# The end of global attention: two of VectorE's new jobs in the last two units

## The chip, the cores and the metric

The kernel runs on one core of a Trainium2 chip. A core has five engines that run their own instruction streams and wait for one another by semaphores: TensorE (PE in the profile: matmul, with its weight loads as PEld), VectorE (DVE), ScalarE (ACT), GpSimd (POOL) and SyncE (SP, which here issues all DMAs). The metric is the time of one execution on the device in microseconds, as a median of runs; lower is better.

## The reference, cut to what matters

Two layers of a diffusion block over 1024 latent tokens and 256 context tokens, width 1024. Each layer projects the normalised tokens into three groups of heads, multiplies each branch by its gate, and projects the concatenation back. The branch that matters here is the global attention: 8 query heads of 64 that share 2 key/value heads, over all 1280 keys.

```python
def dense_attn(q, k, v):
    s = jnp.einsum("bqkgd,bskd->bkgqs", q, k).astype(jnp.float32)
    p = jax.nn.softmax(s, axis=-1).astype(v.dtype)
    o = jnp.einsum("bkgqs,bskd->bqkgd", p, v)
    return o.reshape(o.shape[0], o.shape[1], -1)
...
for l in range(DEPTH):
    ...
    aq, ak, av, ag, bz, bg, nq, nk, nv, ng = jnp.split(h @ w_in[l], SPLIT_POINTS, axis=-1)
    ...
    a_out = global_gqa(aq, ak, av, ak_c, av_c)
    ...
    y = jnp.concatenate([a_out * silu(ag), b_out * silu(bg), n_out * silu(ng)], axis=-1) @ w_out[l]
    ...
    x = x + gate[:, None] * y
```

## The kernel before

Each layer goes through its stages in order: the input projection in parts, the neighbourhood attention in 128-token units, the global attention, and the output projection. The change is in the global attention, which is the same code in both layers.

**The work of a unit.** The global attention is cut into 8 units (`gunits`, made by `ga_unit`): 2 halves of the 1024 queries (512 each), times 2 key heads, times 2 pairs of query heads. A unit handles two heads, `hi` 0 and 1. Its 1280 keys are taken in 5 steps `kp` of 256 keys. Scores are computed transposed, with keys on the partitions and queries along the free axis.

- `scores(hi, kp)`: TensorE computes 256 keys by 512 queries into a 128x1024 PSUM tile (L1037 and L1038, `ps_w`, of which there are two). ScalarE turns it into weights with one exponential (L1040, tile `gp`). The weights of a head are then added up over the steps into `gacc`: step 1 adds the weights of steps 0 and 1 (L1045), steps 2, 3 and 4 add theirs to it (L1048). Steps 1 to 3 are added on GpSimd, step 4 on VectorE, and VectorE then folds the two halves of `gacc` (L1050). An addition is called here by its head and step: "head 1, step 3".
- `values(kp, i)`: TensorE multiplies the weights of one step, both heads, into the output tile `ps_c` (L1057). It is issued one step late, between the next step's two scores. After step 4, which comes in the next unit's step 0, ScalarE copies `ps_c` to `gosb` (L1061).
- `finish()`: issued for a unit in step 2 of the next one. TensorE sums `gacc` over the partitions with a matrix of ones (L1066); ScalarE takes the reciprocal as exp of minus ln (L1070, L1071); VectorE mends it by a Newton step (L1073, L1074) and multiplies by the gated output (L1076, tile `gt`); GpSimd multiplies the gate by `gosb` (L1075).
- `store_u`, the last step of `finish`, splits the result `gt` into a leading part and a rest for the output projection: ScalarE copies `gt` into `hh` in TensorE's rounded float32 (L823), and VectorE subtracts that from `gt` into `hl` (L824).

**The shifts.** The softmax's shift for each query comes from maxima that are computed ahead: matmuls into `ps_b` (L1011, L1016) and maxima on VectorE (L1012, L1017), spread over the units before. They run out in the seventh unit (number 6), so that units 6 and 7 have little or none of them.

**Buffers.** The `gp` and `gacc` tiles of all units share seven 128x1024 buffers (tag `prob`, `PB = 7`); an exponential can only write a buffer whose earlier weights have been read by TensorE and added by whichever engine adds them.

**Order.** TensorE runs the instructions in the order in which the code issues them; on the other engines a scheduler has placed them, and each engine runs its own list strictly in order, so that one instruction that waits holds back all behind it. After the last unit the output projection begins with the first block of `w_out`, which was split before the global attention (L1210, L1211 and L1213, `woh` and `wol`); the other seven blocks are loaded (L1188) and split into two parts by ScalarE (L291) and VectorE (L292).

Of the kernel before, what the change touches and what calls it, by code (L numbers as in the profile page):

```python
# [11 lines left out]
ALU = mybir.AluOpType  # L12
# [62 lines left out]
def hybrid_block_kernel(  # L75
# [8 lines left out]
    PE, ACT, DVE, POOL, SP = nc.tensor, nc.scalar, nc.vector, nc.gpsimd, nc.sync  # L84

    def pool(name, bufs=1, space=None, side=None):
        kw = {}
        if space is not None:
            kw["space"] = space
        if space is not DRAM:  # L90
            kw["reuse_waits"] = "tile"
        if side is not None:
            kw["side"] = side
        return tc.tile_pool(name=name, bufs=bufs, **kw)
# [30 lines left out]
    def ps_one(name):  # L125
        wide.b += 1
        return ps_b[wide.b % 3]

    def ps_acc(name):
        return ps_c  # L130
# [241 lines left out]
    def load_parts(t, src, h, cols, top=0):  # L372

        for kind in range(2):
            i = kind ^ top
            SP.dma_start(out=t[i * 64:(i + 1) * 64].bitcast(F32), in_=head(src, h, kind, cols))

    for l in range(DEPTH):
# [114 lines left out]
        if l:  # L493
# [3 lines left out]
            for i in range(2):  # L497
                pr = ps_pair("ps_feat")
# [97 lines left out]
        for t in range(ntq):  # L596
            ps = proj_tok(W, t, 256)
            g = wp.tile([P, 512], F32, name="gate", bufs=2)
# [215 lines left out]
            g()  # L814


        def store_u(f, t0, n, u, eng=DVE):

            dst = hh[:, f, t0:t0 + n]
            if eng is POOL:  # L820
                POOL.tensor_copy(out=dst, in_=u)
            else:
                ACT.activation(out=dst, in_=u, func=AF.Copy)  # L823
            eng.tensor_tensor(out=hl[:, f, t0:t0 + n], in0=u, in1=dst.bitcast(F32), op=ALU.subtract)  # L824

        def pool_u(f, t0, n):
            u = ap_.tile([P, 512], F32, name="fin", tag="fin", bufs=4)
            SP.dma_start(out=u[:, :n], in_=upd[f, :, t0:t0 + n])
            store_u(4 + f, t0, n, u[:, :n])
# [147 lines left out]
        def gk(g):  # L977
            if g not in gks:
                gks[g] = load_gk(g)
            return gks[g]  # L980


        def ga_unit(cc, g, pr):
            f = 2 * g + pr
            cs = slice(cc * 512, (cc + 1) * 512)
            st = _Env()

            st.q1, st.q2 = (hh[:, f, cs], hl[:, f, cs]), [None] * 2
            st.p, st.acc = {}, [None] * 2

            def load():
                for hi in range(2):
                    load_parts(st.q1[hi], qad, 2 * f + hi, cs)

            def load2():
                for hi in range(2):
                    st.q2[hi] = ak_.tile([P, 512], F32R, name="gq", tag="q", bufs=QB)
                    load_parts(st.q2[hi], qad, 2 * f + hi, cs)

            def shift(i):  # L1000

                hi, j = divmod(i, 10)
                if i == 0:
                    load2()
                    st.mx = small.tile([P, 2, 4, 3], F32, tag="gmx", name="gmx")
                q1, mx = st.q1[hi], st.mx[:, hi]
                k1 = gk(g)[0]
                S = ps_one("ps_m")
                if j < 8:
                    qt, half = divmod(j, 2)  # L1010
                    PE.matmul(S, q1[:, qt * P:(qt + 1) * P], k1[:, half * 512:(half + 1) * 512], start=True, stop=True)  # L1011
                    DVE.reduce_max(out=mx[:, qt, half:half + 1], in_=S, axis=AX.X)  # L1012
                    return
                q0 = 2 * (j - 8)
                for i in range(2):
                    PE.matmul(S[:, i * 256:(i + 1) * 256], q1[:, (q0 + i) * P:(q0 + i + 1) * P], k1[:, SEQ:NT], start=True, stop=True)  # L1016
                DVE.reduce_max(out=mx[:, q0:q0 + 2, 2], in_=S.rearrange("p (a b) -> p a b", a=2), axis=AX.X)  # L1017
                if hi and j == 9:
                    st.nn = small.tile([P, 8], F32, tag="gnn", name="gnn")
                    DVE.tensor_reduce(out=st.nn, in_=st.mx.rearrange("p h q k -> p (h q) k"), op=ALU.max, axis=AX.X, negate=True)  # L1020

            def shift_rows():

                T = ps_one("ps_mt")
                PE.transpose(T[0:8, 0:P], st.nn, ident)
                r = ak_.tile([8, P], F32R, name="gmr", bufs=2)
                ACT.activation(out=r, in_=T[0:8, 0:P], func=AF.Copy)
                for hi in range(2):
                    SP.dma_start(out=st.q2[hi][0:1, :].rearrange("o (i p) -> o i p", p=P).bitcast(F32),
                                 in_=r[4 * hi:4 * hi + 4, :].bitcast(F32))  # L1030

            def scores(hi, kp):
                k1, k2 = gk(g)
                S = ps_pair("ps_st").rearrange("p (a b) -> p a b", a=2)
                for i in range(2):
                    kc = slice((2 * kp + i) * P, (2 * kp + i + 1) * P)
                    PE.matmul(S[:, i, :], k1[:, kc], st.q1[hi], start=True, stop=False)  # L1037
                    PE.matmul(S[:, i, :], k2[:, kc], st.q2[hi], start=False, stop=True)  # L1038
                p = ap_.tile([P, 2, 512], F32, name="gp", tag="prob", bufs=PB)
                ACT.activation(out=p, in_=S, func=AF.Exp)  # L1040
                st.p[hi, kp] = p
                pf = p.rearrange("p a b -> p (a b)")
                if kp == 1:
                    st.acc[hi] = ap_.tile([P, 1024], F32, name="gacc", tag="prob", bufs=PB)
                    POOL.tensor_tensor(out=st.acc[hi], in0=st.p[hi, 0].rearrange("p a b -> p (a b)"), in1=pf, op=ALU.add)  # L1045
                elif kp > 1:
                    eng = DVE if kp == 4 else POOL
                    eng.tensor_tensor(out=st.acc[hi], in0=st.acc[hi], in1=pf, op=ALU.add)  # L1048
                if kp == 4:
                    DVE.tensor_tensor(out=st.acc[hi][:, 0:512], in0=st.acc[hi][:, 0:512], in1=st.acc[hi][:, 512:1024], op=ALU.add)  # L1050

            def values(kp, i):
                if kp == 0 and i == 0:
                    st.o = ps_acc("ps_go")
                kt = 2 * kp + i
                for hi in range(2):
                    PE.matmul(st.o[hi * 64:(hi + 1) * 64, :], av[:, kt, g * 64:(g + 1) * 64], st.p[hi, kp][:, i, :],  # L1057
                              start=(kt == 0), stop=(kt == NTT - 1))
                if kt == NTT - 1:
                    st.osb = ap_.tile([P, 512], F32, name="gosb", tag="fin", bufs=4)  # L1060
                    ACT.activation(out=st.osb, in_=st.o, func=AF.Copy)  # L1061

            def finish():
                s_ps = ps_one("ps_gs")
                for hi in range(2):
                    PE.matmul(s_ps[hi * 64:(hi + 1) * 64, :], ones, st.acc[hi][:, 0:512], start=True, stop=True)  # L1066
                gt = ap_.tile([P, 512], F32, name="ggate", tag="fin", bufs=4)
                SP.dma_start(out=gt, in_=agd[f, :, cs])
                r0 = ap_.tile([P, 512], F32, name="gr0", tag="fin", bufs=4)
                ACT.activation(out=r0, in_=s_ps, func=AF.Ln)  # L1070
                ACT.activation(out=r0, in_=r0, func=AF.Exp, scale=-1.0)  # L1071
                t1 = ap_.tile([P, 512], F32, name="gt1", tag="fin", bufs=4)
                DVE.tensor_tensor(out=t1, in0=s_ps, in1=r0, op=ALU.mult)  # L1073
                DVE.scalar_tensor_tensor(out=t1, in0=t1, scalar=-2.0, in1=r0, op0=ALU.add, op1=ALU.mult)  # L1074
                POOL.tensor_tensor(out=gt, in0=gt, in1=st.osb, op=ALU.mult)  # L1075
                DVE.scalar_tensor_tensor(out=t1, in0=t1, scalar=-1.0, in1=gt, op0=ALU.mult, op1=ALU.mult)  # L1076
                store_u(f, cc * 512, 512, t1)

            return shift, scores, values, finish, load, shift_rows

        gunits = [ga_unit(cc, g, pr) for cc in range(2) for g in range(2) for pr in range(2)]

        shifts = []
        for i, u in enumerate(gunits):
# [86 lines left out]
        op = opx.enter_context(pool(f"op{l}", side=left))  # L1171
# [48 lines left out]
        for t0, n in ochunks:  # L1220
# [4 lines left out]
            for i in range(n):  # L1225
# [13 lines left out]
                elif last and t == NTL - 1:  # L1239

                    for c0, w in ((0, 512), (512, 256), (768, 256)):
                        ps, cs = ps_one("ps_y"), slice(c0, c0 + w)
                        for k in range(KT):
                            a, b = hh[:, k, ts_], hl[:, k, ts_]
# [7 lines left out]
                else:  # L1252
                    ps, f = proj_out(t)
# [88 lines left out]
```

## Time and profile before

| | us |
|---|---|
| median of 3 runs (1530.3 to 1532.41) | 1530.85 |
| the profiled execution's own time | 1529.36 |
| its span, first to last instruction | 1527.6 |
| TensorE busy | 1467.3 |
| VectorE busy | 864.1 |
| ScalarE busy | 640.7 |
| GpSimd busy | 515.0 |

The time of an execution is 1.8 us longer than the span that the profile covers. Rows of a timeline give the start from the span's beginning, the length, the engine, the line, the operation, the tiles (written <- read), the shapes and how many equal instructions in a row were merged; brackets give the idle time of the engine just ahead and what ended it. A busy share is a mean over stages with different limits, so the stage that the change touches is read by its own rows. In layer 0 the two units concerned and their end lie at about 675 to 722 us of the span, in layer 1 at about 1387 to 1433 us.

### The profile page before, as it was taken

How to read it: one execution, taken by the hardware profiler on the slowest of the kernel's cores; microseconds unless marked ns; L12 is line 12 of the kernel's file. 1: busy time of each engine (PE TensorE's matmuls, PEld its weight loads, DVE VectorE, ACT ScalarE, POOL GpSimd, SP SyncE). 2: the span in 40 equal slices, each digit the busy share in tenths (PEclk: the TensorE clock that was granted, in tenths of full speed). 3: DMA queues.
4: the chain of work that ended last, by engine and by line, in shares of the span. 5: the costliest groups of instructions: out<-in, count | busy, mean ns of one | idle time of the engine just before them, and what ended most of it. 6: DMA issues, size and time to landing. Idle time of an engine off the chain costs nothing.

```text
span 1527.6 us, 22281 instructions
## 1 busy us (share of the span) xinstructions
PE 1467.3 (96%) x8001; PEld 1072.9 (70%) x8001; DVE 864.1 (57%) x1666; ACT 640.7 (42%) x1228; POOL 515.0 (34%) x618
## 2 busy tenths in 40 slices
PE   5999999999999999999999999999999999999999
PEld 3787777788888554544788888878778854544577
DVE  3645344541678678774533553464368768785522
ACT  4643232334676444444312452333466544444400
POOL 0233346000144565564001323460012265665200
PEclk9999999999999999999999999999999999999999
DMA  9447445437745201010512132343796301001331
GB/s 310 149 126 233 130 149 167 148 114 174 196 127 141 66 22 42 21 42 21 179 70 103 61 111 75 90 138 83 180 219 143 105 22 42 21 28 35 140 116 55
DMA packets 153039, 167.91 MB, mean 110 GB/s; under 512 B 35384, under 2 KB 112032, under 8 KB 152864
## 3 DMA queue, kind: packets, MB, share of 16 engines
q1 hardware_dynamic: 152928, 166.48, 37.3%
q8 instruction: 63, 1.03, 0.3%
q14 instruction: 48, 0.39, 0.1%
HBM read 126.45 MB, written 40.86 MB: 110 GB/s over the span
## 4 chain that ended last, share of the span: by engine, by line
PE 51%; DVE 8%; ACT 3%; DMA 2%; issue 2%; POOL 0%; SPq 0%; DVEq 0%; ACTq 0%; POOLq 0%
PE ps_c L1057 8%; PE ps_w L1210 4%; PE ps_w L1213 4%; PE ps_w L1211 4%; PE ps_w L1037 4%; PE ps_w L1038 3%; PE ps_w L423 3%; PE ps_w L424 3%; PE ps_w L422 3%; PE ps_b L1011 3%; DVE gt L1076 2%; DVE gmx L1012 1%; DVE gacc L1048 1%; PE ps_c L902 1%; PE ps_b L1016 1%
## 5 line engine op out<-in xcount | busy, mean ns | idle before, releaser
L1040 ACT ACTIVATE gp<-ps_w 128x1024 f32<-128x1024 f32 x160 | 162.5, 1022 | 190.7 <-PE ps_w L1038 155.1
L422 PE MATMUL ps_w<-wh,hh 128*128 128x512 f32 (+1 forms) x624 | 234.7, 376 | 1.3 <-ACT wh L291 1.3
L423 PE MATMUL ps_w<-wl,hh 128*128 128x512 f32 (+1 forms) x624 | 228.5, 366 | 1.0 <-DVE wl L292 1.0
L424 PE MATMUL ps_w<-wh,hl 128*128 128x512 f32 (+1 forms) x624 | 228.1, 366 | 0.0
L1012 DVE TENSOR_REDUCE gmx<-ps_b 128x1 f32<-128x512 f32 x256 | 171.9, 685 | 72.1 <-PE ps_b L1011 67.9
L1057 PE MATMUL ps_c<-gp,av 128*64 128x512 f32 x640 | 166.6, 614 | 10.2 <-ACT gp L1040 10.1
L1048 POOL TENSOR_TENSOR gacc<-gacc,gp 128x1024 f32<-128x1024 f32 x64 | 161.3, 2549 | 25.8 <-ACT gp L1040 25.5
L422 PEld LDWEIGHTS ps_w<-wh,hh 128*128 128x128 f32 x624 | 117.7, 189 | 25.2 <-issue 2.9
L423 PEld LDWEIGHTS ps_w<-wl,hh 128*128 128x128 f32 x624 | 117.5, 188 | 21.4 <-DVE wl L292 2.2
L424 PEld LDWEIGHTS ps_w<-wh,hl 128*128 128x128 f32 x624 | 117.3, 188 | 21.2
L1038 PE MATMUL ps_w<-gq,kst 128*128 128x512 f32 x320 | 126.7, 396 | 0.0
L1210 PE MATMUL ps_w<-woh,hh 128*128 128x512 f32 x272 | 109.4, 402 | 0.0
L643 DVE TENSOR_REDUCE qss<-sq 128x8 f32<-128x512 f32 (+2 forms) x58 | 31.2, 538 | 135.3 <-ACT sq L641 135.2
L1211 PE MATMUL ps_w<-wol,hh 128*128 128x512 f32 x272 | 107.5, 395 | 0.0
L1057 PEld LDWEIGHTS ps_c<-gp,av 128*64 128x64 f32 x640 | 42.9, 137 | 88.5 <-issue 66.5
L877 POOL TENSOR_SCALAR rg<-ngate,rr 128x64 f32<-128x64 f32 x88 | 28.6, 329 | 225.9 <-PE ps_b L890 106.0
L1045 POOL TENSOR_TENSOR gacc<-gp 128x1024 f32<-128x1024 f32 x32 | 75.8, 2370 | 49.8 <-ACT gp L1040 49.8
L292 DVE TENSOR_TENSOR wl<-wraw,wh 128x512 fp32r<-128x512 f32 (+1 forms) x96 | 66.6, 713 | 35.1 <-ACT wh L291 33.7
L1213 PE MATMUL ps_w<-woh,hl 128*128 128x512 f32 x272 | 85.6, 396 | 0.0
L874 ACT ACTIVATE prob<-ps_w,m 128x768 f32<-128x768 f32 (+2 forms) x88 | 72.7, 826 | 25.6 <-DVE m L861 12.5
L430 PE MATMUL ps_w<-hh,wh 128*128 128x512 f32 (+1 forms) x208 | 80.7, 388 | 0.8 <-ACT wh L291 0.8
L432 PE MATMUL ps_w<-hh,wl 128*128 128x512 f32 (+1 forms) x208 | 78.9, 379 | 0.0
(226 smaller groups left out, 2973.7 us busy)
## 6 DMA issues: line engine op xcount, KB each, us to landing
wmod<-in_w_mod_dram SPq DMA_DIRECT2D x48, 512.0 KB
wraw<-in_w_in_dram SPq DMA_DIRECT2D x64, 256.0 KB
gq<-qad SPq DMA_DIRECT2D x64, 128.0 KB
woraw<-in_w_out_dram SPq DMA_DIRECT2D x14, 512.0 KB
wraw<-in_w_in_dram SPq DMA_DIRECT2D x48, 128.0 KB
kst<-knd SPq DMA_DIRECT2D x16, 320.0 KB
qad<-qklo SPq DMA_DIRECT2D x18, 256.0 KB
qad<-qkhi SPq DMA_DIRECT2D x18, 256.0 KB
```

The source lines that it names most:

```text
L422: PE.matmul(ps[:, :n], a, wh[:, off:off + n], start=(k == 0), stop=False)
L423: PE.matmul(ps[:, :n], a, wl[:, off:off + n], start=False, stop=False)
L424: PE.matmul(ps[:, :n], b, wh[:, off:off + n], start=False, stop=(k == KT - 1))
L430: PE.matmul(ps[:, :n], wh[:, fs], hh[:, k, ts_], start=(k == 0), stop=False)
L1012: DVE.reduce_max(out=mx[:, qt, half:half + 1], in_=S, axis=AX.X)
L1038: PE.matmul(S[:, i, :], k2[:, kc], st.q2[hi], start=False, stop=True)
L1040: ACT.activation(out=p, in_=S, func=AF.Exp)
L1048: eng.tensor_tensor(out=st.acc[hi], in0=st.acc[hi], in1=pf, op=ALU.add)
L1057: PE.matmul(st.o[hi * 64:(hi + 1) * 64, :], av[:, kt, g * 64:(g + 1) * 64], st.p[hi, kp][:, i, :], start=(kt == 0), stop=(kt == NTT - 1))
L1210: PE.matmul(ps[:, i2, :], a, oh[:, cs], start=(k == 0), stop=False)
L1211: PE.matmul(ps[:, i2, :], a, ol[:, cs], start=False, stop=False)
L1213: PE.matmul(ps[:, i2, :], b, oh[:, i2 * 512:(i2 + 1) * 512], start=False, stop=(k == KT - 1))
```

## The change

Two things move to VectorE, in both layers.

1. The copy of the result into `hh` (L823) moves from ScalarE to VectorE for the units numbered 5 and 6, counting from 0. Their `finish` is issued in step 2 of the next unit, so the copies stand in units 6 and 7: the last two. Unit 7's own `finish`, which comes after the last unit, keeps its copy on ScalarE.
2. Additions of weights move from GpSimd to VectorE for head 1: all of steps 1, 2 and 3 in unit 7, and step 3 in unit 6. Step 4 was on VectorE before. Head 0 keeps its additions on GpSimd up to step 3.

```diff
-        def store_u(f, t0, n, u, eng=DVE):
+        def store_u(f, t0, n, u, eng=DVE, cp=None):
             dst = hh[:, f, t0:t0 + n]
-            if eng is POOL:
-                POOL.tensor_copy(out=dst, in_=u)
+            if eng is POOL or cp:
+                (cp or eng).tensor_copy(out=dst, in_=u)
             else:
                 ACT.activation(out=dst, in_=u, func=AF.Copy)
             eng.tensor_tensor(out=hl[:, f, t0:t0 + n], in0=u, in1=dst.bitcast(F32), op=ALU.subtract)
...
-        def ga_unit(cc, g, pr):
+        def ga_unit(n, cc, g, pr):
...
+            def add_eng(hi, kp):
+
+                return DVE if kp == 4 or (hi and (n == 7 or (n == 6 and kp == 3))) else POOL
+
             def scores(hi, kp):
...
-                    POOL.tensor_tensor(out=st.acc[hi], in0=st.p[hi, 0].rearrange("p a b -> p (a b)"), in1=pf, op=ALU.add)
+                    add_eng(hi, kp).tensor_tensor(out=st.acc[hi], in0=st.p[hi, 0].rearrange("p a b -> p (a b)"), in1=pf, op=ALU.add)
                 elif kp > 1:
-                    eng = DVE if kp == 4 else POOL
-                    eng.tensor_tensor(out=st.acc[hi], in0=st.acc[hi], in1=pf, op=ALU.add)
+                    add_eng(hi, kp).tensor_tensor(out=st.acc[hi], in0=st.acc[hi], in1=pf, op=ALU.add)
...
-                store_u(f, cc * 512, 512, t1)
+                store_u(f, cc * 512, 512, t1, cp=DVE if n in (5, 6) else None)
...
-        gunits = [ga_unit(cc, g, pr) for cc in range(2) for g in range(2) for pr in range(2)]
+        gunits = [ga_unit(4 * cc + 2 * g + pr, cc, g, pr) for cc in range(2) for g in range(2) for pr in range(2)]
```

How the instructions stand on each engine follows from a scheduler, so three places are shown. All are in layer 1's last two units; layer 0 reads the same. The line numbers after the change are higher by three or four: the exponential L1040 is L1044, the additions L1045 and L1048 are L1049 and L1051, the fold L1050 is L1053, and the lines of `finish` go up by three.

ScalarE before, from unit 7's exponentials of step 2 to its last one (the copy of unit 6's result is the row with `hh`):

```order
L1040 ACTIVATE gp<-ps_w_10537 128x1024
L1070 ACTIVATE gr_13099<-ps_b_71 128x512
L1071 ACTIVATE gr_13099<-gr_13099 128x512
L1040 ACTIVATE gp<-ps_w_10536 128x1024
L823 ACTIVATE hh<-gt_13102 128x512
L1040 ACTIVATE gp<-ps_w_10537 128x1024
L1040 ACTIVATE gp<-ps_w_10536 128x1024
L1040 ACTIVATE gp<-ps_w_10537 128x1024
L1061 ACTIVATE gosb<-ps_c 128x512
```

After the change, at the same place:

```order
L1044 ACTIVATE gp<-ps_w_10537 128x1024
L1073 ACTIVATE gr_13099<-ps_b_71 128x512
L1074 ACTIVATE gr_13099<-gr_13099 128x512
L1044 ACTIVATE gp<-ps_w_10536 128x1024
L1044 ACTIVATE gp<-ps_w_10537 128x1024
L1044 ACTIVATE gp<-ps_w_10536 128x1024
L1044 ACTIVATE gp<-ps_w_10537 128x1024
L1064 ACTIVATE gosb<-ps_c 128x512
```

Nothing stands any longer between the exponential of head 0, step 3 and that of head 1, step 3.

VectorE in unit 7, before: unit 6's end, and then the step-4 additions with their folds.

```order
L1073 TENSOR_TENSOR gt_13102<-ps_b_71,gr_13099 128x512
L1074 SCALAR_TENSOR_TENSOR gt_13102<-gt_13102,gr_13099 128x512
L1076 SCALAR_TENSOR_TENSOR gt_13102<-gt_13102,ggate 128x512
L824 TENSOR_TENSOR hl<-gt_13102,hh 128x512
L1048 TENSOR_TENSOR gacc<-gacc,gp 128x1024
L1050 TENSOR_TENSOR gacc<-gacc 128x512
L1048 TENSOR_TENSOR gacc<-gacc,gp 128x1024
L1050 TENSOR_TENSOR gacc<-gacc 128x512
```

After:

```order
L1049 TENSOR_TENSOR gacc<-gp 128x1024
L1051 TENSOR_TENSOR gacc<-gacc,gp 128x1024
L1076 TENSOR_TENSOR gt_13102<-ps_b_71,gr_13099 128x512
L1077 SCALAR_TENSOR_TENSOR gt_13102<-gt_13102,gr_13099 128x512
L1079 SCALAR_TENSOR_TENSOR gt_13102<-gt_13102,ggate 128x512
L821 CAST hh<-gt_13102 128x512
L824 TENSOR_TENSOR hl<-gt_13102,hh 128x512
L1051 TENSOR_TENSOR gacc<-gacc,gp 128x1024 x2
L1053 TENSOR_TENSOR gacc<-gacc 128x512
L1051 TENSOR_TENSOR gacc<-gacc,gp 128x1024
L1053 TENSOR_TENSOR gacc<-gacc 128x512
```

Head 1's additions of steps 1 and 2 stand ahead of unit 6's end, the copy (CAST) inside it, and head 1's step 3 behind it, ahead of head 0's step 4; in all, four more instructions ahead of the last fold.

GpSimd, units 6 and 7, before and then after:

```order
L1045 TENSOR_TENSOR gacc<-gp 128x1024 x2
L1048 TENSOR_TENSOR gacc<-gacc,gp 128x1024 x4
L1075 TENSOR_TENSOR ggate<-ggate,gosb 128x512
L1045 TENSOR_TENSOR gacc<-gp 128x1024 x2
L1048 TENSOR_TENSOR gacc<-gacc,gp 128x1024 x4
L1075 TENSOR_TENSOR ggate<-ggate,gosb 128x512
```

```order
L1049 TENSOR_TENSOR gacc<-gp 128x1024 x2
L1051 TENSOR_TENSOR gacc<-gacc,gp 128x1024 x3
L1078 TENSOR_TENSOR ggate<-ggate,gosb 128x512
L1049 TENSOR_TENSOR gacc<-gp 128x1024
L1051 TENSOR_TENSOR gacc<-gacc,gp 128x1024 x2
L1078 TENSOR_TENSOR ggate<-ggate,gosb 128x512
```

One addition has left unit 6, three have left unit 7. TensorE's and SyncE's lists are the same as before but for line numbers.

## The prediction

> **What bounds the kernel now.** First the page: TensorE is busy for 96% of the span, so time can only go where TensorE stands still.
>
> ```profile
> span 1527.6 us, 22281 instructions
> PE 1467.3 (96%) x8001; PEld 1072.9 (70%) x8001; DVE 864.1 (57%) x1666; ACT 640.7 (42%) x1228; POOL 515.0 (34%) x618
> ```
>
> Then TensorE's waits: the end of layer 0's global attention (640 to 725 us), that of layer 1's (1360 to 1434 us), and what follows layer 0's (722 to 1000 us). Columns: us in total, times, longest.
>
> ```profile
> PE ps_c L1057 <- ACT gp L1040: 5.0, 2, 3.1
> ...
> PE ps_c L1057 <- ACT gp L1040: 5.2, 3, 3.1
> PE ps_b L1066 <- DVE gacc L1050: 0.5, 1, 0.5
> ...
> PE ps_w L422 <- ACT wh L291: 0.8, 1, 0.8
> ```
>
> In each layer TensorE's products with the weights wait twice for ScalarE's exponential, and behind that it hardly waits. TensorE's timeline shows where; layer 1, and at the foot two rows of layer 0:
>
> ```profile
> 1395.31 1.07 PE L1057 MATMUL ps_c<-gp,av 128*64 128x512 f32 x2
> 1398.24 1.93 PE L1057 MATMUL ps_c<-gp,av 128*64 128x512 f32 x6 [1.86 <-ACT gp L1040]
> 1400.11 0.50 PE L1037 MATMUL ps_w<-hl,kst 128*128 128x512 f32 x1
> 1402.15 2.25 PE L1057 MATMUL ps_c<-gp,av 128*64 128x512 f32 x8
> 1414.87 0.49 PE L1037 MATMUL ps_w<-hh,kst 128*128 128x512 f32 x1
> 1419.90 1.07 PE L1057 MATMUL ps_c<-gp,av 128*64 128x512 f32 x2
> 1424.09 3.53 PE L1057 MATMUL ps_c<-gp,av 128*64 128x512 f32 x6 [3.11 <-ACT gp L1040]
> 1427.54 0.55 PE L1037 MATMUL ps_w<-hl,kst 128*128 128x512 f32 x1
> 1432.39 1.07 PE L1066 MATMUL ps_b<-gacc,ones 128*64 128x512 f32 x2 [0.49 <-DVE gacc L1050]
> 1433.39 0.50 PE L1210 MATMUL ps_w<-woh,hh 128*128 128x512 f32 x1
> ...
> 683.05 1.07 PE L1057 MATMUL ps_c<-gp,av 128*64 128x512 f32 x2
> 721.79 0.50 PE L1210 MATMUL ps_w<-woh,hh 128*128 128x512 f32 x1
> ```
>
> A group of eight L1057 that isn't held up takes 2.2 us (1402.15). The step-3 group of unit 6 is torn: two go at 1395.31, six at 1398.24. That of unit 7 is torn further, and its six take 3.53 instead of 1.93 us. ScalarE shows the cause:
>
> ```profile
> 1396.65 0.63 ACT L823 ACTIVATE hh<-gt 128x512 fp32r<-128x512 f32 x1 [4.07 <-DVE gt L1076]
> 1397.19 1.92 ACT L1040 ACTIVATE gp<-ps_w 128x1024 f32<-128x1024 f32 x2
> 1409.78 1.03 ACT L1040 ACTIVATE gp<-ps_w 128x1024 f32<-128x1024 f32 x1 [2.22 <-PE ps_w L1038]
> 1413.33 1.94 ACT L1040 ACTIVATE gp<-ps_w 128x1024 f32<-128x1024 f32 x2 [2.52 <-POOL gacc L1045]
> 1416.33 1.01 ACT L1040 ACTIVATE gp<-ps_w 128x1024 f32<-128x1024 f32 x1
> 1422.49 0.63 ACT L823 ACTIVATE hh<-gt 128x512 fp32r<-128x512 f32 x1 [5.15 <-DVE gt L1076]
> 1423.03 1.92 ACT L1040 ACTIVATE gp<-ps_w 128x1024 f32<-128x1024 f32 x2
> 1428.89 1.02 ACT L1040 ACTIVATE gp<-ps_w 128x1024 f32<-128x1024 f32 x1 [3.94 <-PE ps_w L1038]
> ```
>
> The copy L823 waits 4.07 and 5.15 us for VectorE's L1076, and head 1's step-3 exponential, whose scores have long been done, stands behind it. And L1076 is late because of GpSimd (VectorE's rows, then GpSimd's):
>
> ```profile
> 1416.46 0.69 DVE L1073 TENSOR_TENSOR gt<-ps_b,gr 128x512 f32<-128x512 f32 x1 [11.99 <-ACT gr L1071]
> 1417.18 2.52 DVE L1074 SCALAR_TENSOR_TENSOR gt<-gt,gr 128x512 f32<-128x512 f32 x1
> 1419.80 2.65 DVE L1076 SCALAR_TENSOR_TENSOR gt<-gt,ggate 128x512 f32<-128x512 f32 x1
> 1425.05 2.56 DVE L1048 TENSOR_TENSOR gacc<-gacc,gp 128x1024 f32<-128x1024 f32 x1 [1.20 <-ACT gp L1040]
> 1430.38 1.22 DVE L1048 TENSOR_TENSOR gacc<-gacc,gp 128x1024 f32<-128x1024 f32 x1 [2.05 <-ACT gp L1040]
> 1431.64 0.69 DVE L1050 TENSOR_TENSOR gacc<-gacc 128x512 f32<-128x512 f32 x1
> ...
> 1410.95 2.35 POOL L1045 TENSOR_TENSOR gacc<-gp 128x1024 f32<-128x1024 f32 x1 [0.94 <-ACT gp L1040]
> 1414.43 7.47 POOL L1048 TENSOR_TENSOR gacc<-gacc,gp 128x1024 f32<-128x1024 f32 x3 [1.14 <-ACT gp L1040]
> ```
>
> L1073, with one operand in PSUM, takes 0.69 us beside a busy GpSimd. L1074 and L1076, with both operands in SBUF, take 2.5 and 2.65, and L1076 ends 0.55 us after GpSimd's third addition (1421.90). The same addition on VectorE takes 2.56 us or, with GpSimd idle, 1.22. So the two take turns, a whole instruction at a time; L1074 and L1076 unhindered would take about 0.69. On GpSimd an addition takes 2.35.
>
> The granted clock (sixth figure, between busy times and DMA share) tells why the six were slow: after the 1.9 us of unit 6 it stays at 1.00, after the 3.1 us of unit 7 it falls to about half for some microseconds.
>
> ```profile
> 1389.00:1402.00 13.00, 11.13 (x43) 4.95 (x41) 9.84 (x9) 6.21 (x9) 9.43 (x4) 1.00 0.29 101
> 1424.00:1428.00 4.00, 3.92 (x8) 1.07 (x9) 2.92 (x2) 0.95 (x2) 2.35 (x1) 0.57 0.02 4
> 714.00:718.00 4.00, 4.00 (x7) 1.46 (x6) 2.08 (x2) 0.34 (x1) 0.31 (x1) 0.54 0.00 0
> ```
>
> **The change part by part.** Layer 1 first, in the times of this span.
>
> *Copy off ScalarE, unit 6.* The exponential of head 1, step 3 can go when its scores are done, about 1394.5 (they end ahead of the group at 1395.31), and ends at 1395.5. The group then runs through: 1395.3 + 2.2 = 1397.5, and the next scores start there instead of at 1400.11. Gain 2.6 us.
>
> *Copy off ScalarE, unit 7.* All is 2.6 earlier, so the group starts at 1417.3 and its exponential ends at about 1417.4. It ends at 1417.3 + 2.2 = 1419.5, where head 1's step-4 scores started at 1427.54: 8.0 us gained so far, of which 3.1 was the wait and 1.6 the halved clock.
>
> *Additions to VectorE, and the waits that they add.* In unit 7 the exponential of head 0, step 2 needs a buffer that head 1's step-1 addition has read. That was GpSimd's 1410.95 row, the 2.52 us wait of 1413.33. Now it is VectorE's: the weights end at 1408.2 (1409.78 + 1.03 - 2.6), 1.22 us make 1409.5, and the exponential runs until 1410.5. Behind it on ScalarE stand head 1's step 2 and unit 6's reciprocal. TensorE needs its PSUM tile for the scores at 1412.3 (1414.87 - 2.6): 1.8 us of cover. The other buffers that VectorE now frees are those of unit 6's head 1, done by about 1402, some 2 us and more ahead of use. If this cover went, each microsecond would be one on TensorE.
>
> *VectorE's tail.* This sets the end, since the last sums (L1066) need the last fold (L1050). GpSimd's last addition of unit 7, head 0's step 3, starts when its weights are there. Their scores start at 1412.3 and end some 1.1 later; with 1.0 of exponential that is 1414.5, and the addition ends at 1416.9. VectorE first adds head 1's step 2 (behind GpSimd's addition of head 0's step 2, 1410.5 to 1412.9), until 1414.2, then L1073 until 1414.9, when GpSimd is at work again: L1074 must wait, and ends at 1416.9 + 0.55 = 1417.45. From there GpSimd is idle and nothing is in the way. With 0.05 us between instructions: L1076 0.69 (1418.2), the copy 0.45 (1418.7), L824 0.69 (1419.45), head 1's step 3 1.22 (1420.7), head 0's step 4 1.22 (1421.95), its fold 0.69 (1422.7), head 1's step 4 1.22 (1423.95), the fold 0.69 (1424.7). From last fold to first L1210 it was 1433.39 - (1431.64 + 0.69) = 1.06 us; so L1210 starts at 1425.75. Gain in layer 1: 1433.39 - 1425.75 = 7.6 us.
>
> The copy's price has no row. The nearest above is a VectorE copy out of PSUM, below it an operation with one SBUF operand on twice the elements:
>
> ```profile
> L893 DVE COPY probt<-ps_b 128x512 f32<-128x512 f32 x16 | 10.8, 677 | 2.3 <-PE ps_b L890 2.2
> L256 DVE TENSOR_SCALAR xt<-xt,rs_y 128x1024 f32<-128x1024 f32 x10 | 7.2, 749 | 0.1
> ```
>
> Half of 749 ns is 0.37; so 0.37 to 0.68 us. I take 0.45, near L256, whose operands lie in the same memory. The other end costs 0.2 us a layer.
>
> *Layer 0.* The same order, 1395.31 - 683.05 = 712.26 us earlier, so L1210 would start at 1425.75 - 712.26 = 713.5 instead of 721.79: 8.3 us. It is more because the clock stayed low for longer there.
>
> *Behind the units.* The eight blocks of `w_out`, their splits and the output are released by what stands around the first L1210 and move with it; the only wait shown behind layer 0 was 0.8 us. I charge nothing; a gain lost there is a rival.
>
> Sum: 7.6 + 8.3 = 15.9 us. The profiled execution took 1529.36 (span 1527.6, and 1.8 around it), which makes 1513.5. The median before is 1530.85, 1.5 above that execution; against the median it is 1530.85 - 15.9 = 1514.9.
>
> **The rivals.** *VectorE gets its turn first* (0.11): L1074 slips in ahead of GpSimd's last addition, which it misses by about 0.5 us in my sum, and the tail is 2.4 us shorter. Then TensorE is the limit: the last exponential ends 1.35 + 1.02 us after the scores' start (1428.89 against 1427.54), at 1421.9; last products and sums bring L1210 to about 1424.5. Gain 8.9 + 9.5 = 18.4: 1512.4. Against it: GpSimd needs only the exponential, VectorE two operations.
>
> *VectorE loses one turn more, or the gain is lost in part later* (0.11): one more collision costs 2.35 us a layer and stretches TensorE's wait for the fold, about 1.2 us in my sum, to 3.5, past the 3.1 that halved the clock: 1.6 more. So 4 us a layer: 15.9 - 8 = 8 gained, 1523. If layer 0's or layer 1's gain were lost to a later `w_out` load, it would be 1523 as well.
>
> *VectorE becomes the bound* (0.04): if all seven two-operand instructions of the tail met GpSimd, four additions would cost 1.34 more each (2.56 - 1.22) and L1076 and L824 1.9 each: 9.2 us, L1210 at 1434.9 and 722.7, and the clock halved behind it, 1.6 a layer. That is 1.5 + 0.9 + 3.2 = 5.6 us slower, 1536.5. It decides from five or six collisions a layer; against it, GpSimd has only three additions left in unit 7, and is idle in the tail. [...]
>
> *Nothing comes of it* (0.02): another wait ends where the old did, 1530.5.
>
> **How the numbers follow.** The forecast, both torn groups whole and VectorE's tail as summed, has 0.72. The predicted time is its 1515, on its own 1513 to 1517 (the copy's bounds, and 1 us a layer for starts read off rows). The range runs from 1511, below the first rival, to 1521, the forecast with three more microseconds lost in each layer; it leaves out the second rival, the slower case and the one without gain, 0.17 together. Faster by over 0.2% (3 us, about what a measurement tells apart here) are forecast and the first two rivals, 0.94; within it 0.02; slower 0.04.
>
> **What would show it.** In the timeline after, the step-3 groups of units 6 and 7 should be whole (eight in 2.2 us), with no L823 between exponentials and the clock at 1.00. Unit 6's L1074 and unit 7's should still be stretched, the copy at about 0.45. TensorE's last wait for the fold should grow from 0.5 to about 1.2 us. The span from unit 6's group to L1210 should be 30.4 us in both layers (38.1 and 38.7 before). A torn group, or several additions of 2.5 us on VectorE behind unit 7's L1076, would make it wrong.

## The result, and the profile after

| | before | after |
|---|---|---|
| median of four runs each, side by side, us | 1531.63 (1530.3 to 1533.77) | 1514.60 (1511.32 to 1516.31) |
| the profiled execution's own time, us | 1529.36 | 1513.59 |
| from unit 6's step-3 group of products to the first matmul of the output projection, layer 0 | 38.74 | 30.14 |
| the same, layer 1 | 38.08 | 30.10 |

The ratio of the times is 0.9888, with a 95% interval from 0.987 to 0.9907. The change makes the kernel 1.1% faster, 17.0 us by these medians and 15.8 us by the two profiled executions.

The page after has TensorE 10.2 us less busy than before (1467.3), though it runs the same 8001 matmuls. In the two stretches of the table its busy time fell from 66.0 to 58.4 us: a torn group of products counts 3.0 us (1.07 + 1.93) where a whole one takes 2.2, and the halved clock makes up most of the rest. The other 2.6 us lie outside the stretches, mainly ahead of the first one, where the two executions differ without the change's doing.

```profile
span 1511.8 us, 22274 instructions
PE 1457.1 (96%) x8001; PEld 1071.0 (71%) x8001; DVE 866.0 (57%) x1678; ACT 639.5 (42%) x1224; POOL 495.6 (33%) x610
```

TensorE's waits after, for the same three stretches as before: the end of layer 0's global attention, that of layer 1's, and what follows layer 0's (us in total, times, longest).

```profile
PE ps_b L1069 <- DVE gacc L1053: 0.7, 1, 0.7
PE ps_c L1060 <- ACT gp L1044: 0.2, 1, 0.2
...
PE ps_b L1069 <- DVE gacc L1053: 0.8, 1, 0.8
PE ps_c L1060 <- ACT gp L1044: 0.2, 1, 0.2
...
PE ps_w L422 <- ACT wh L291: 0.9, 1, 0.9
```

The products' wait for the exponential was 5.0 and 5.2 us and is 0.2 in each layer. The last sums' wait for the fold has grown from 0.5 to 0.8 in layer 1; in layer 0, where none is listed before, it is 0.7. What follows layer 0 waits 0.9 where it waited 0.8, so nothing was given back there. TensorE's timeline, layer 1 and at the foot two rows of layer 0:

```profile
1387.52 2.18 PE L1060 MATMUL ps_c<-gp,av 128*64 128x512 f32 x8
1389.63 0.50 PE L1041 MATMUL ps_w<-hl,kst 128*128 128x512 f32 x1
...
1409.43 2.19 PE L1060 MATMUL ps_c<-gp,av 128*64 128x512 f32 x8
1411.55 0.50 PE L1041 MATMUL ps_w<-hl,kst 128*128 128x512 f32 x1
...
1416.62 1.07 PE L1069 MATMUL ps_b<-gacc,ones 128*64 128x512 f32 x2 [0.76 <-DVE gacc L1053]
1417.62 0.50 PE L1213 MATMUL ps_w<-woh,hh 128*128 128x512 f32 x1
...
683.58 2.19 PE L1060 MATMUL ps_c<-gp,av 128*64 128x512 f32 x8
713.72 0.50 PE L1213 MATMUL ps_w<-woh,hh 128*128 128x512 f32 x1
```

Both step-3 groups are whole: eight products in 2.2 us, where two went before and six after a wait. The granted clock (the sixth figure) stays at full speed through both ends, where it was at 0.54 and 0.57:

```profile
1405.00:1420.00 15.00, 14.06 (x53) 6.57 (x52) 12.05 (x12) 7.52 (x11) 3.95 (x3) 1.00 0.17 54
700.00:714.00 14.00, 13.10 (x49) 5.43 (x46) 11.74 (x11) 6.55 (x9) 5.05 (x3) 1.00 0.18 56
```

ScalarE's exponentials of steps 2 and 3 of unit 7 (the middle row is head 0, step 2, which needs a buffer; the last row is both heads of step 3, with nothing between them), then VectorE's list from unit 7's first addition to the last fold, and GpSimd's last addition:

```profile
1401.76 1.02 ACT L1044 ACTIVATE gp<-ps_w 128x1024 f32<-128x1024 f32 x1 [1.42 <-DVE gacc L1049]
1408.61 1.95 ACT L1044 ACTIVATE gp<-ps_w 128x1024 f32<-128x1024 f32 x2 [1.90 <-PE ps_w L1042]
...
1400.44 1.23 DVE L1049 TENSOR_TENSOR gacc<-gp 128x1024 f32<-128x1024 f32 x1 [5.28 <-ACT gp L1044]
1404.61 1.77 DVE L1051 TENSOR_TENSOR gacc<-gacc,gp 128x1024 f32<-128x1024 f32 x1 [2.94 <-ACT gp L1044]
1406.31 0.68 DVE L1076 TENSOR_TENSOR gt<-ps_b,gr 128x512 f32<-128x512 f32 x1
1407.02 2.78 DVE L1077 SCALAR_TENSOR_TENSOR gt<-gt,gr 128x512 f32<-128x512 f32 x1
1409.83 0.69 DVE L1079 SCALAR_TENSOR_TENSOR gt<-gt,ggate 128x512 f32<-128x512 f32 x1
1410.55 0.43 DVE L821 CAST hh<-gt 128x512 fp32r<-128x512 f32 x1
1411.01 0.69 DVE L824 TENSOR_TENSOR hl<-gt,hh 128x512 fp32r<-128x512 f32 x1
1411.62 2.35 DVE L1051 TENSOR_TENSOR gacc<-gacc,gp 128x1024 f32<-128x1024 f32 x2
1414.01 0.69 DVE L1053 TENSOR_TENSOR gacc<-gacc 128x512 f32<-128x512 f32 x1
1414.62 1.22 DVE L1051 TENSOR_TENSOR gacc<-gacc,gp 128x1024 f32<-128x1024 f32 x1
1415.87 0.69 DVE L1053 TENSOR_TENSOR gacc<-gacc 128x512 f32<-128x512 f32 x1
...
1406.85 2.39 POOL L1051 TENSOR_TENSOR gacc<-gacc,gp 128x1024 f32<-128x1024 f32 x1 [1.55 <-ACT gp L1044]
```

L1077 still waits for GpSimd's addition (it ends at 1409.80, the addition at 1409.24). Behind it GpSimd is idle up to 1416.56, and every VectorE instruction takes its unhindered time (0.69 us on 128x512, 1.2 on 128x1024). The copy, now a CAST on VectorE, takes 0.43 us.

The two gains, 8.60 and 7.98, make 16.6 us, 0.8 more than the executions differ by. The rest is outside: layer 0's stretch began 0.53 us later in the span (683.58 for 683.05), and the way from layer 0's first output matmul to layer 1's stretch took 673.80 for 673.52.

### The profile page after: what moved, and what is told of

Same layout as the page of the kernel before. It is cut to its first block, busy times and chain, and to the rows that moved or that the text cites. A ratio compares the mean times of both kernels' runs of the same rounds, so it can differ in the third digit from the quotient of the medians.

```text
span 1511.8 us, 22274 instructions
## 1 busy us (share of the span) xinstructions
PE 1457.1 (96%) x8001; PEld 1071.0 (71%) x8001; DVE 866.0 (57%) x1678; ACT 639.5 (42%) x1224; POOL 495.6 (33%) x610
## 4 chain that ended last, share of the span: by engine, by line
PE 52%; DVE 8%; DMA 2%; issue 2%; ACT 2%; SPq 1%; POOL 0%; DVEq 0%; ACTq 0%
PE ps_c L1060 8%; PE ps_w L1213 4%; PE ps_w L1216 4%; PE ps_w L1214 4%; PE ps_w L1041 4%; PE ps_w L1042 4%; PE ps_w L423 3%; PE ps_w L424 3%; PE ps_w L422 3%; PE ps_b L1011 3%; DVE gacc L1051 2%; DVE gmx L1012 1%; DVE gt L1079 1%; PE ps_c L902 1%; PE ps_b L1016 1%
## 5 line engine op out<-in xcount | busy, mean ns | idle before, releaser
L1044 ACT ACTIVATE gp<-ps_w 128x1024 f32<-128x1024 f32 x160 | 162.8, 1022 | 193.3 <-PE ps_w L1042 159.5
L1012 DVE TENSOR_REDUCE gmx<-ps_b 128x1 f32<-128x512 f32 x256 | 171.8, 685 | 72.1 <-PE ps_b L1011 67.9
L1060 PE MATMUL ps_c<-gp,av 128*64 128x512 f32 x640 | 159.8, 605 | 0.3 <-ACT gp L1044 0.3
L1051 POOL TENSOR_TENSOR gacc<-gacc,gp 128x1024 f32<-128x1024 f32 x58 | 146.5, 2552 | 24.3 <-ACT gp L1044 24.1
L1213 PE MATMUL ps_w<-woh,hh 128*128 128x512 f32 x272 | 109.5, 403 | 0.0
L1049 POOL TENSOR_TENSOR gacc<-gp 128x1024 f32<-128x1024 f32 x30 | 71.1, 2371 | 47.5 <-ACT gp L1044 47.5
```

Of the source, the lines that this page charges most:

```text
L1051: add_eng(hi, kp).tensor_tensor(out=st.acc[hi], in0=st.acc[hi], in1=pf, op=ALU.add)
L1213: PE.matmul(ps[:, i2, :], a, oh[:, cs], start=(k == 0), stop=False)
```

## The experiments

The theory: an exponential stood on ScalarE behind a copy that waited for VectorE, VectorE waited for GpSimd, and the second of these waits halved TensorE's clock (0.54 in layer 0, 0.57 in layer 1); the copy's move ends the waits, and the additions' move keeps VectorE from ending late. The rivals: the copy alone does it all, or the additions alone do; the halved clock is not a cost of its own; VectorE is now nearly the bound. "Stretch" below is that of the table above, in layer 0 and in layer 1. The runs of the first four experiments stood beside 18 runs of the kernel before (median 1530.93), those of the others beside 17 (1529.65).

**The copy alone.** The additions go back to where they were.

```diff
-                return DVE if kp == 4 or (hi and (n == 7 or (n == 6 and kp == 3))) else POOL
+                return DVE if kp == 4 else POOL
```

> Only the copy of the result goes to VectorE for units 5 and 6; all additions up to step 3 stay on GpSimd. The measure is the stretch from the start of unit 6's step-3 group of products to the first matmul of the output projection: 38.1 us in layer 1 and 38.7 in layer 0 before, 30.1 in both with the whole change. Theory (the copy on ScalarE tears the groups, the additions only set VectorE's tail): both groups whole, but L1077 and L1079 of unit 7 each wait for a GpSimd addition, the last fold comes some 2 us later and TensorE waits about 3 us for it: 32 to 33 us a layer, 10 to 13 us gained in all, some 1519. Rival one (the copy is everything): 30.1 a layer, 16 gained, 1515. Rival two (what helps is GpSimd's relief): a group is still torn, 36 a layer or more, under 5 gained.

Measured: 1524.81 us, ratio 0.9956 (0.9939 to 0.9972); stretch 34.51 and 33.57, so 4.2 and 4.5 us gained. The groups are whole, but the end is later than expected, and the time misses the expected 1519 by 6 us. VectorE and GpSimd in layer 1's unit 7:

```profile
1414.22 2.52 DVE L1077 SCALAR_TENSOR_TENSOR gt<-gt,gr 128x512 f32<-128x512 f32 x1
1416.84 2.67 DVE L1079 SCALAR_TENSOR_TENSOR gt<-gt,ggate 128x512 f32<-128x512 f32 x1
1419.55 2.47 DVE L821 CAST hh<-gt 128x512 fp32r<-128x512 f32 x1
...
1424.52 2.29 DVE L1051 TENSOR_TENSOR gacc<-gacc,gp 128x1024 f32<-128x1024 f32 x1
...
1411.47 10.27 POOL L1051 TENSOR_TENSOR gacc<-gacc,gp 128x1024 f32<-128x1024 f32 x4 [1.14 <-ACT gp L1044]
1424.08 1.65 POOL L1078 TENSOR_TENSOR ggate<-ggate,gosb 128x512 f32<-128x512 f32 x1 [2.34 <-ACT gosb L1064]
```

GpSimd runs four additions back to back, and VectorE gets one instruction in per addition: L1077, L1079 and the copy start 2.6 to 2.7 us apart. The copy takes 2.47 instead of 0.43. Even the last step-4 addition meets GpSimd, now at the gate's product, and takes 2.29 instead of 1.22. So TensorE's last sums wait for two folds:

```profile
1424.66 1.07 PE L1069 MATMUL ps_b<-gacc,ones 128*64 128x512 f32 x2 [1.29 <-DVE gacc L1053]
1427.59 1.07 PE L1069 MATMUL ps_b<-gacc,ones 128*64 128x512 f32 x2 [1.86 <-DVE gacc L1053]
...
719.00:722.00 3.00, 3.00 (x8) 2.33 (x9) 1.55 (x2) 3.00 (x5) 0.00 (x0) 0.50 0.00 0
1429.00:1432.00 3.00, 3.00 (x9) 2.35 (x8) 1.72 (x2) 3.00 (x5) 0.00 (x0) 0.50 0.00 0
```

The same two waits stand in layer 0, and in both layers the clock was halved behind them (the last two rows, layer 0 and layer 1). Most of that cost lies behind the stretch, which ends at the first output matmul. From there to the seventh L1213 that reads `woh` and `hh` it took 5.97 us in layer 0 and 5.85 in layer 1, where the kernel before took 4.31 and 4.30 (its L1210). So 3.2 of the 8.7 us gained in the stretches are lost again, and 5.5 are left; the medians differ by 6.1. The copy's move alone thus exchanges the torn groups for a late tail and a halved clock: it is a third of the gain.

**The additions alone.** The copy stays on ScalarE.

```diff
-                store_u(f, cc * 512, 512, t1, cp=DVE if n in (5, 6) else None)
+                store_u(f, cc * 512, 512, t1)
```

> Only the additions of head 1 go to VectorE; the copy stays on ScalarE. Theory: unit 6's group stays torn as before (1.9 us of wait), since its L1077 and L1079 meet the same GpSimd additions. In unit 7 only one GpSimd addition stands in their way, the copy is ready 1.5 us sooner, the wait falls from 3.1 to about 1.5 us and the clock isn't halved: 34 to 35 us in each layer, 7 to 9 us gained in all, some 1523. Rival one (the copy is everything): both groups torn as before, 0 to 2 us gained. Rival two (GpSimd's relief is everything): 30.1 a layer, 16 gained.

Measured: 1523.77 us, ratio 0.9957 (0.9941 to 0.9972); stretch 34.59 and 34.82, so 4.15 and 3.3 us gained, as expected. Layer 1's two groups are still torn, but the second wait is short:

```profile
1392.06 1.93 PE L1060 MATMUL ps_c<-gp,av 128*64 128x512 f32 x6 [2.15 <-ACT gp L1044]
1416.45 1.93 PE L1060 MATMUL ps_c<-gp,av 128*64 128x512 f32 x6 [1.64 <-ACT gp L1044]
```

The six products take 1.93 us in both, and the granted clock around unit 7's is 1.00 in both layers (704 to 711 and 1412 to 1419 us), so no clock was halved. The output projections start at their usual pace: 4.31 us to the seventh L1213 in each layer. The additions alone thus gain 7.4 us in both layers together (7.2 by the medians). With the copy's 5.5 that makes 12.9, against 16.6 for the whole; by the medians it is 13.3, against some 17. The whole is worth more than its parts: once the copy has moved, the additions also take away the late tail and the halved clock behind it.

**The copy on GpSimd.** The whole change, but with the copy on GpSimd. It tells whether VectorE matters as the copy's place, or only that the copy is off ScalarE.

```diff
-                store_u(f, cc * 512, 512, t1, cp=DVE if n in (5, 6) else None)
+                store_u(f, cc * 512, 512, t1, cp=POOL if n in (5, 6) else None)
```

> As the whole change, but the copy of units 5 and 6 goes to GpSimd, where it stands behind the last addition of the unit. Theory (what counts is that no exponential stands behind the copy, not which engine makes it): both groups whole, VectorE's subtraction L824 waits some 0.3 to 0.8 us longer for the copy: 30.1 to 31 us a layer, 14.5 to 16.5 gained, 1514.5 to 1517. Rival (VectorE's fast copy matters, GpSimd's is slow and holds VectorE off by the shared turn): 32 us or more a layer, under 13 gained.

Measured: 1516.63 us, ratio 0.9901 (0.9885 to 0.9916); stretch 30.35 and 30.33, groups whole, 0.8 us of wait for the fold. A copy took 0.61 us on GpSimd as a mean of four. The stretch is 0.2 us longer than with the change and the gain, 14.3 us, just below the expected 14.5. So it hardly matters which of the two engines copies.

**Matmuls in the second wait.** The kernel before, with eight more matmuls between the two and the six products of unit 7, where TensorE waits. They write a PSUM tile that nothing reads; nothing of the computation is changed. If the wait itself were the whole cost, this would gain nothing; if the halved clock is a cost of its own, the six should run at full speed.

```diff
             for hi in range(2):
+                if hi and kt == 6 and cc and g and pr:
+                    fill_ps = ps_one("ps_fill")
+                    for _ in range(8):
+                        PE.matmul(fill_ps, gk(g)[0][:, 0:P], gk(g)[0][:, 0:512], start=True, stop=True)
                 PE.matmul(st.o[hi * 64:(hi + 1) * 64, :], av[:, kt, g * 64:(g + 1) * 64], st.p[hi, kp][:, i, :],
```

> The kernel before, with eight matmuls whose result nobody reads, put into unit 7's torn group ahead of its first product for head 1, where TensorE waits 3.1 us in each layer. They take some 1.9 us and fill the wait. Theory (the idle halved the clock): the six products behind the wait take 1.9 us again, layer 1's stretch falls from 38.1 to 36.5 and layer 0's from 38.7 to about 36.3, 3.5 to 4.5 us gained though work is added. Rival (the products were slow for another reason, such as contention): no gain, or up to 1 us lost.

Measured: 1526.63 us, ratio 0.9973 (0.9961 to 0.9984); stretch 37.78 and 36.47. In this kernel the products are L1061. Unit 6 of layer 0, with its clock, and unit 7 of layer 1:

```profile
685.86 3.36 PE L1061 MATMUL ps_c<-gp,av 128*64 128x512 f32 x6 [1.88 <-ACT gp L1040]
...
1422.92 1.93 PE L1061 MATMUL ps_c<-gp,av 128*64 128x512 f32 x6 [1.11 <-ACT gp L1040]
...
686.00:689.00 3.00, 3.00 (x6) 0.52 (x4) 2.18 (x1) 0.72 (x1) 2.30 (x1) 0.53 0.24 94
```

Unit 7's six run in 1.93 instead of 3.53 us, at a granted clock of 1.00 from 1420 to 1428 us, with 1.11 us of wait left, and layer 1's stretch is 1.6 us shorter, just the sum that was put down to the halved clock: it is a cost of its own. In layer 0 unit 7's six take 1.93 us as well, where they took 3.68. Layer 0's stretch missed its expectation by 1.5 us, because unit 6's six ran slow there, behind a wait of 1.88 us. The kernel before has the same wait at the same place, at full clock:

```profile
686.00 1.93 PE L1057 MATMUL ps_c<-gp,av 128*64 128x512 f32 x6 [1.88 <-ACT gp L1040]
...
683.00:690.00 7.00, 5.12 (x18) 2.17 (x18) 5.07 (x4) 3.30 (x4) 3.18 (x2) 1.00 0.53 189
```

So here the length of a wait alone didn't decide whether the clock fell: behind 1.88 us it was 0.53 once and 1.00 once.

**The change once more,** beside the runs that follow.

> The whole change once more, beside the three runs that build on it. All theories: 14 to 18 us less than before, the stretch from unit 6's step-3 group to the output projection 30.1 us in both layers.

Measured: 1512.88 us, ratio 0.9894 (0.9875 to 0.9913); stretch 30.13 in both layers.

**Unit 6's end one step earlier.** If VectorE's tail still sets the end, taking work out of it should take away the 0.8 us of wait.

```diff
-                if kp == 2 and pv:
+                if kp == (1 if i == nu - 1 else 2) and pv:
```

> The whole change, and unit 6's finish is issued in step 1 of unit 7 instead of step 2. Theory (VectorE's tail, not TensorE's own work, sets the last 0.8 us of each layer's stretch): the reciprocal, L1077, L1079, the copy and L824 are done ahead of the step-3 additions, the last fold comes some 0.7 us sooner, TensorE's wait for it goes from 0.8 to about 0: 29.3 to 29.6 us a layer, 1 to 1.6 less than the whole change. Rival (the reciprocal on ScalarE, now ahead of the step-2 exponentials, holds up products): a group is torn again, 30.5 us a layer or more.

Measured: 1512.40 us, ratio 0.9885 (0.9866 to 0.9905); stretch 29.52 and 29.46, as expected, and no wait for a fold.

**All of unit 7's additions on VectorE.** GpSimd then has none left in unit 7. If VectorE were near to being the bound, this would cost; if the turns with GpSimd were the price, it would gain.

```diff
-                return DVE if kp == 4 or (hi and (n == 7 or (n == 6 and kp == 3))) else POOL
+                return DVE if kp == 4 or n == 7 or (hi and n == 6 and kp == 3) else POOL
```

> The whole change, and head 0's additions of unit 7 go to VectorE as well, so that GpSimd makes none there. Theory (VectorE is late by its turns with GpSimd, some 2.6 us, more than the one addition of 1.2 us that falls into the tail costs): L1077 and head 1's step-2 addition take 0.7 and 1.2 us instead of 2.8 and 1.8, the last fold is sooner, and TensorE's wait for it about 0: 29.3 to 29.6 us a layer, 1 to 1.6 less than the whole change. Rival (VectorE is at its limit): the last fold is later, 30.5 to 32 us a layer, 1 to 4 more.

Measured: 1511.95 us, ratio 0.9888 (0.9868 to 0.9907); stretch 29.38 and 29.34, as expected. L1077 takes 0.69 us here, where the change has 2.78:

```profile
1407.06 0.69 DVE L1077 SCALAR_TENSOR_TENSOR gt<-gt,gr 128x512 f32<-128x512 f32 x1
```

Three more additions of 1.22 us cost VectorE nothing, because it no longer waits its turn. By the traces this and the experiment before are 0.6 to 0.8 us a layer better than the change; the times of the runs can't tell the three apart.

**The copy on VectorE for the earlier units too.** If a waiting copy on ScalarE cost something in every unit, this would gain.

```diff
-                store_u(f, cc * 512, 512, t1, cp=DVE if n in (5, 6) else None)
+                store_u(f, cc * 512, 512, t1, cp=DVE if n < 7 else None)
```

> The whole change, with the copy on VectorE for units 0 to 4 too. Theory (the copy on ScalarE costs where no shift matmuls cover it, and VectorE is full of maxima in the units before): nothing gained in units 1 to 5, where TensorE already waits 1.2 us a layer for a maximum; that wait grows by up to 2 us: 0 to 4 us more than the whole change. Rival (the copy tears groups in every unit): 2 us or more gained.

Measured: 1532.07 us, ratio 1.0017 (1.0005 to 1.0029): the whole gain is gone, about 19 us above the change in the same company, though the stretch is as good as with the change (30.14 and 30.10). Neither expectation had this. The copies' group on VectorE (count, busy time, mean in ns), then unit 1 of layer 1 on VectorE, GpSimd and TensorE, and its clock:

```profile
L821 DVE CAST hh<-gt 128x512 fp32r<-128x512 f32 x14 | 21.6, 1542 | 0.1
...
1259.50 1.99 DVE L821 CAST hh<-gt 128x512 fp32r<-128x512 f32 x1
...
1253.23 7.97 POOL L1051 TENSOR_TENSOR gacc<-gacc,gp 128x1024 f32<-128x1024 f32 x3
...
1262.87 0.50 PE L1011 MATMUL ps_b<-kst,hh 128*128 128x512 f32 x1 [0.77 <-DVE gmx L1012]
1264.60 0.50 PE L1011 MATMUL ps_b<-kst,hh 128*128 128x512 f32 x1 [1.24 <-DVE gmx L1012]
1266.54 3.20 PE L1060 MATMUL ps_c<-gp,av 128*64 128x512 f32 x8
...
1266.00:1270.00 4.00, 4.00 (x13) 1.42 (x13) 3.28 (x5) 1.23 (x2) 0.00 (x0) 0.61 0.00 0
```

The ten copies of the earlier units take 1.99 us each (21.6 less four of 0.43, over ten), the one shown beside GpSimd's additions. In these units VectorE also has the shifts' maxima (L1012), on which TensorE's matmuls into `ps_b` (L1011) wait for a free tile. So the maxima are late. Here TensorE waits twice, for 0.77 and 1.24 us, and the clock fell behind that: eight products take 3.20 us instead of the 1.94 of the groups around. The kernel with the change has a single wait at this place:

```profile
1257.76 0.50 PE L1011 MATMUL ps_b<-kst,hh 128*128 128x512 f32 x1 [1.21 <-DVE gmx L1012]
```

Over both global attentions, TensorE's waits for maxima, and for a load of queries (`gq`) that had come in time before, grew by 7.8 us, and its busy time by 10.5 us over the whole span (1467.6 for 1457.1). That is 2.4 more than the spans differ by (1527.7 for 1511.8). Most of this was made up at the program's start, where TensorE's last group behind a load of `wmod` began 1.9 us sooner (46.27 for 48.18).

## Why the prediction was right, point by point

- **The time.** 1515 was forecast and 1514.6 measured; by the profiled executions 15.9 us of gain were forecast and 15.8 came. That it is so close is in part luck: the stretches gained 0.7 us more than forecast and the rest of the execution lost 0.8, and the four runs of the change alone lie 5 us apart.
- **Unit 6's copy.** Forecast 2.6 us gained; from group to next scores it went from 4.80 (1400.11 - 1395.31) to 2.11 us, 2.7 gained.
- **Unit 7's copy.** Forecast 8.0 up to head 1's step-4 scores, unit 6's 2.6 included; from 32.23 (1427.54 - 1395.31) to 24.03 (1411.55 - 1387.52), 8.2 gained. Of this, 3.1 as a wait and 1.6 as a halved clock were separated rightly: the added matmuls gave back the 1.6 alone. The 0.7 us in each unit that the sum took in but didn't name is the torn group itself (3.0 us of products for 2.2).
- **The new wait for a buffer.** The exponential of head 0, step 2 waits for VectorE's addition now (1.42 us) and ends at 1402.78. The sum had 1410.5, which is 1402.7 in the time of this span (7.79 earlier). TensorE didn't notice.
- **VectorE's tail.** GpSimd's last addition was put at 1414.5 to 1416.9, that is 1406.7 to 1409.1, and ran from 1406.85 to 1409.24. L1077 missed its turn as forecast and ended at 1409.80 (1409.66 forecast). But it missed it by 0.17 us (1407.02 for 1406.85), where the sum had about 0.5: the first rival was nearer than the sum made it.
- **What was mis-sized.** Behind it the sum had 7.25 us to the end of the last fold, and it took 6.76. The term of 0.05 us between instructions was too much: some start 0.08 us before the last one's end (1411.62 behind 1411.01 + 0.69). So the wait for the fold is 0.76 and not 1.2 us, and the stretch 30.1 and not 30.4. The copy's 0.45 was 0.43.
- **Layer 0.** 8.3 forecast, 8.6 came, for the same reason.
- **Nothing lost behind.** The wait behind layer 0 is 0.9 us, 0.8 before.
- **The rivals.** VectorE getting its turn first did not happen, but the run with all of unit 7's additions on VectorE comes close to it, with L1077 at 0.69 us and no wait for a fold: 29.4 us a stretch (the rival's sum makes 29.2), 1.5 us less than the change over both layers, where the rival had put 2.5 less than the forecast. A late tail with several turns lost, and a halved clock behind it, did show in the copy alone. VectorE as the bound is refuted for unit 7 by three more additions that cost nothing.
- **Where the reasoning was too simple.** The prediction tied the halved clock to the wait's length: "after the 1.9 us of unit 6 it stays at 1.00, after the 3.1 us of unit 7 it falls". The runs show 1.88 us that halved it (0.53) and 1.88 us that didn't (1.00). So a wait's length didn't settle it. The second rival's surcharge of 1.6 us a layer was of the right size (the copy alone lost 1.7 and 1.6 that way), but it came there behind two shorter waits and not behind one of 3.5.

The additions' part was underrated in words: the prediction costed them in VectorE's tail and never said what the copy's move would do without them. It would have been a third of the gain.

## What to carry to other kernels

Look for an instruction that waits in a strictly ordered engine list ahead of one that the bottleneck needs; moving it can save the bottleneck the whole wait (here 5.0 and 5.2 us a layer became 0.2), and here two engines with nothing urgent behind it did nearly equally well as its new place (stretches of 30.1 and 30.3 us). Follow the wait one engine further, though: here it came from VectorE and GpSimd taking turns, and taking GpSimd's work out of the tail was worth more than moving the copy (7.4 us for 5.5), and both together more than their sum. A stretch that is measured must reach to where the clock is full again, or a halved clock behind a wait goes uncounted, as 3.2 us did in the copy alone. The same move was a loss in the earlier units, where VectorE also had the maxima (about 19 us above the change), so decide it by unit and not by line.

## What was unexpected of the hardware

**The length of one wait didn't decide whether the clock fell.** A wait of 1.88 us left it at 1.00 in the kernel before and halved it (0.53) at the same place in the run with the added matmuls, which stand in a later unit. One of 2.15 us in the additions alone left the products behind it at full speed (1.93 us). Two waits of 1.29 and 1.86 us, with a microsecond of matmuls between, halved it (0.50) in both layers of the copy alone: in layer 0 from the matmuls right behind them (1.97 us for 1.07), in layer 1 from a microsecond later. Behind two of 0.77 and 1.24 us it was 0.61 over 4 us. What made equal waits end differently, no run here shows.

**A copy on VectorE between two SBUF tiles took 0.43 us alone and 2 to 2.5 us beside GpSimd.** It reads only one tile, and the prediction's range for it (0.37 to 0.68) had no such case. Beside running additions it ended just behind GpSimd's last one: by 0.28 us in the copy alone (1422.02 for 1421.74, 2.47 us long), by 0.29 in the run with all the copies on VectorE (1261.49 for 1261.20, 1.99 us long). The change was spared this because GpSimd had no additions left there: the last had ended at 1409.24, and the copy started at 1410.55.
